# A hybrid decoder layer on one core: first token tiles on ScalarE's queue, one gate half moved forward, token loads four ahead, MLP operand copies pinned in program order

## The chip, the cores and the metric

The kernel runs on one core of a Trainium2 chip. The metric is the device time of one execution in microseconds, lower being better; the times shown are medians of several runs. The core has TensorE (matmuls; weight loads are listed apart as PEld), VectorE (DVE), ScalarE (ACT), GpSimd (POOL) and SyncE (SP). SP, ScalarE and GpSimd each have a queue on which they issue DMAs.

## The reference, cut to what matters

One layer of a decoder, batch 1, 512 tokens, model width 1024, f32:

```python
h = rms_norm(x, norm_mix)
rq, rk, rv, rg, cq, ckv, krope, gr, gm = split(h @ w_in)
a_ret = (rms_norm(retention(rope(rq), rope(rk) / 16, rv)) * silu(rg)) @ w_br   # 4 heads
q  = rms_norm(cq) @ w_uq;  k, v = split(rms_norm(ckv) @ w_ukv)                 # 8 heads
a_mla = causal_attention(rope(rms_norm(q)), rope(rms_norm([k, krope])), v) @ w_bm
x = x + (sigmoid(gr) * a_ret + sigmoid(gm) * a_mla) @ w_o
x = x + square(relu(rms_norm(x) @ w_up)) @ w_down                              # 4096 wide
x = x + sigmoid(rms_norm(x) @ w_ple_gate) * (p @ w_ple)
```

## The kernel before, in words

**Number format.** Every f32 operand is split into a high part (ScalarE rounds it, `ACT(hi, ..., AF.Copy)`) and a low part (VectorE subtracts: `lo = raw - hi`). A product is three matmuls: low weights by high tokens, high by low and high by high (`mm3`, line 292; all matmuls are issued through line 169). So each weight chunk costs a DMA (`prepare`, 218), a ScalarE copy (`wh`, line 262) and a VectorE subtraction (`wl`, 266), and each activation the same pair in `split` (302 to 314).

**Order of the work.** `step(key, fn, ...)` calls at the end of the kernel write the program's order; `run_steps` (271) walks them, and at each step that needs a weight chunk it converts chunks up to one ahead (AHEAD = 1) and starts DMAs up to three ahead (PREP = 3). Converted chunks share NW = 3 buffers, raw ones NRAW = 6. A planner then orders each engine's instructions: by program order among those that it takes to be ready by its own costs. `MM` pins all matmuls in program order. `tc.keep_in_program_order(i)` pins an instruction behind the one written just before it for the same engine; before the change it holds on ScalarE for the first chunks (`a1`), the first tokens, sines and sigmoids.

**Stages that the change touches.**
- The head (361 to 392): nine matmuls on a zero tile (364), then for k = 0 to 7 a weight chunk `a1 k` and a token tile `xs[k]`, both loaded on SP's queue in turn, the gains `gn` on ScalarE's queue, then constants and positions on SP's. `first_products` (385) multiplies them into three PSUM banks `pA`.
- The attention (1193 to 1271). Between its short dependent parts lie 26 fillers, halves of the gate products `gm` and `gr` (`gate_m` 679, `gate_r` 889); `fill(n)` places the next n of them, and the last call places what is left. The first half of a gate opens a PSUM bank, the second half scales it and sends it to DRAM on GpSimd's queue. Around the change the order is `query_rotary` (pqa, pqb), `mask_parts`, `rotary_out` (VectorE work on pqa and pqb), two fillers, `rotary_key` (it begins with the transposes `prho`), one filler, and so on.
- The bm stage (1272 to 1280): `norm_x` (708) loads token tile k once more on SP's queue, scales and splits it; it is called once ahead of every `branch_m` step.
- The MLP (1349 to 1395): group 0 of `up` in plain form, then groups in a seven-product form. `down` of group g and `up_seven` of group g+1 alternate in the order "1 v3 7 u1 2 6 u7 5 4 u6 3 u2 u5 u4": a bare number p is a down product (`dn`, two chunks of 24 matmuls in all), `up` a product of the next group (`us`, 48 matmuls, two chunks). `up_operand(p)` (996) makes the tokens of product p (`xu p`) and is called after "2", "5", "4", "3" and "u2" for p = 6, 2, 5, 4 and 3. `down_out` (1095) copies p = 1, 7, 6, 3 of group 0 out of PSUM on ScalarE (`d`, 1103). `up_seven` copies p = 1, 7, 6 out on ScalarE (`f`, 1042).

Of the kernel before, what the change touches and what calls it, by code (L numbers as in the profile page):

```python
# [33 lines left out]
AF = mybir.ActivationFunctionType  # L34
# [3 lines left out]
P = 128  # L38
# [110 lines left out]
def trunk_layer(ctx: ExitStack, tc: tile.TileContext, xT, pT, pos, gains, const, decay, wstream, outT):  # L149
    nc = tc.nc  # L150
# [15 lines left out]
    ACT = nc.scalar.activation  # L166

    def MM(*a, **k):
        return tc.keep_in_program_order(nc.tensor.matmul(*a, **k))  # L169

    def T(name, dtype=F32):
        return dyn.tile([P, S], dtype, tag="t", name=name)

    def K(name, dtype=F32):
        return keep.tile([P, S], dtype, tag="k", name=name)

    def B(name):
        return psum.tile([P, S], F32, tag="ps", name=name)
# [5 lines left out]
    gn = cpool.tile([P, G_N], F32, tag="gn", name="gn")  # L184
# [8 lines left out]
    def g(col):  # L193
        return gn[:, col:col + 1]
# [13 lines left out]
    def step(key, fn, *args):  # L208
        steps.append((key, fn, args))
# [8 lines left out]
    def prepare(key):  # L218

        if key[0] == "sw":  # L220
            _, blk, p, c = key

            def more(raw, kb, fb):
                nc.gpsimd.dma_start(raw, chunk(("w", blk, kb, fb, c)), accum_op=ALU.add)  # L224

            if p in (6, 4):
                return more(dw[blk, "t", c], *((0, 0) if p == 6 else (1, 0)))
            kb, fb = {1: (0, 0), 7: (0, 1), 2: (1, 0), 5: (0, 1), 3: (1, 1)}[p]
            nm = f"{blk[0]}{blk[1]}{p}{c}"
            if p == 7 and blk[0] in ("dn", "up"):  # L230
                raw = tail_pool["w"].tile([P, 1024], F32, tag="draw", name="dr_" + nm, bufs=NDRAW)
            else:
                raw = wpool.tile([P, 1024], F32, tag="wraw", name="wr_" + nm, bufs=NRAW)
            nc.sync.dma_start(raw, chunk(("w", blk, kb, fb, c)))
            dw[blk, "t" if p == 7 else p, c] = raw
            if p == 7:
                more(raw, 1, 1)
            elif p == 5:
                more(raw, 0, 0)
            return  # L240
        width = spec[key][0]
        nm = "_".join(str(x) for x in key)
        raw = wpool.tile([P, width], F32, tag="wraw", name="wr_" + nm, padded_shape=[P, 1024], bufs=NRAW)
        tc.keep_in_program_order(nc.sync.dma_start(raw, chunk(key))) if key[0] == "a1" else nc.sync.dma_start(raw, chunk(key))
        dw[key] = raw

    def load_chunk(key):

        sign = 1.0
        if key[0] == "sw":  # L250
            _, blk, p, c = key
            raw = dw[blk, "t" if p in (7, 6, 4) else p, c]
            nm = f"{blk[0]}{blk[1]}{p}{c}"
            if p in (1, 4) and blk[0] not in ("dn", "up"):
                sign = -1.0
        else:
            raw = dw[key]
            nm = "_".join(str(x) for x in key)
        width = raw.shape[-1]
        hi = wpool.tile([P, width], F32R, tag="whi", name="wh_" + nm, padded_shape=[P, 1024])  # L260
        lo = wpool.tile([P, width], F32R, tag="wlo", name="wl_" + nm, padded_shape=[P, 1024])
        i = ACT(hi, raw, AF.Copy, scale=sign)  # L262
        if key[0] == "a1":
            tc.keep_in_program_order(i)
        if sign > 0:
            TT(lo, raw, hi.bitcast(F32), op=ALU.subtract)  # L266
        else:
            STT(lo, raw, sign, hi.bitcast(F32), op0=ALU.mult, op1=ALU.subtract)
        wt[key] = (hi, lo)
# [22 lines left out]
    def mm3(ps, stat, mov, first, last, **k):  # L292

        (sh, sl), (mh, ml) = stat, mov
        MM(ps, sl, mh, start=first, stop=False, **k)
        MM(ps, sh, ml, start=False, stop=False, **k)
        MM(ps, sh, mh, start=False, stop=last, **k)

    def cut(pair, a, n=P):
        return pair[0][:, a:a + n], pair[1][:, a:a + n]  # L300

    def split(src, name, scale=None, hi=None, lo=None, pin=False):

        hi = T(name + "h", F32R) if hi is None else hi
        lo = T(name + "l", F32R) if lo is None else lo
        if scale is None:
            ACT(hi, src, AF.Copy)
            TT(lo, src, hi.bitcast(F32), op=ALU.subtract)  # L308
        else:
            i = ACT(hi, src, AF.Copy, scale=scale)  # L310
            if pin:
                tc.keep_in_program_order(i)
            STT(lo, src, scale, hi.bitcast(F32), op0=ALU.mult, op1=ALU.subtract)  # L313
        return hi, lo
# [35 lines left out]
    V = {}  # L350
# [10 lines left out]
    zero = K("zero", F32R)  # L361
    nc.vector.memset(zero.bitcast(F32), 0.0)
    ps = B("zero")
    for i in range(9):
        MM(ps, zero[:, 0:P], zero, start=i == 0, stop=i == 8)
    xs, xg = [], []
    for k in range(8):
        xs.append(T(f"x{k}"))
        if k < 6:
            prepare(("a1", k))  # L370
        tc.keep_in_program_order(nc.sync.dma_start(xs[k], xT[:, k]))
    nc.scalar.dma_start(gn, gains)
    tc.keep_in_program_order(nc.sync.dma_start(cst, const))
    tc.keep_in_program_order(nc.sync.dma_start(posi, pos.partition_broadcast(P)))
    for k in range(8):
        if k >= 6:
            prepare(("a1", k))
        load_chunk(("a1", k))
        xg.append(split(xs[k], f"xg{k}", g(G_MIX + k), pin=True))
# [5 lines left out]
    def first_products(w, k):  # L385
        if k == 0:
            V["pA"] = [B(f"pA{n}") for n in range(3)]
        for n in range(3):
            mm3(V["pA"][n], cut(w, n * P), xg[k], k == 0, k == 7)
        ACT(xs[k], xs[k], AF.Square)  # L390
        if k:
            TT(xs[0], xs[0], xs[k], op=ALU.add)
# [312 lines left out]

    xr, xn, XS = [], [], {}

    def norm_x(k):

        t = T(f"xr{k}")  # L710
        nc.sync.dma_start(t, xT[:, k])
        STT(t, t, g(G_MIX + k), V["rbc"], op0=ALU.mult, op1=ALU.mult)
        xr.append(t)
        xn.append(split(t, f"xn{k}"))

    def x_operand(p):
# [239 lines left out]
    def A(name, shape, tag, bufs, dtype=F32):  # L956
        return tail_pool["a"].tile([P, *shape], dtype, tag=tag, name=name, bufs=bufs)
# [38 lines left out]
    def up_operand(p):  # L996

        f1, f2 = F["x", 0], F["x", 1]
        a11, a21, a12, a22 = f1[:, :, 0:256], f1[:, :, 256:512], f2[:, :, 0:256], f2[:, :, 256:512]
        if p == 7:  # L1000
            TT(a11, a21, a11, op=ALU.subtract)
        elif p == 6:
            TT(a11, a22, a11, op=ALU.subtract)
            TT(a21, a21, a22, op=ALU.subtract)
        elif p == 3:
            TT(a11, a12, a11, op=ALU.subtract)
        src = {1: a11, 7: a11, 6: a11, 3: a11, 2: a12, 5: a21, 4: a22}[p]
        scale = -1.0 if p in (1, 4) else None
        XU[p], pairs = [], ([], [])
        for i, tiles in enumerate(pairs):  # L1010
            nm = f"xu{p}{'hl'[i]}"
            if p in (1, 7) or (p, i) == (6, 0):
                t = A(nm, (4, 256), "xs", 5, F32R)
                tiles.extend((t[:, 0:2], t[:, 2:4]))
                continue
            for c in range(2):

                t = K(f"{nm}{c}", F32R) if p != 6 else keep.tile([P, S], F32R, tag=("sum", "bc")[c], name=f"{nm}{c}", bufs=1)
                tiles.append(t.rearrange("p (k c) -> p k c", k=2))
        for c, (hi, lo) in enumerate(zip(*pairs)):  # L1020
            split(src[:, 2 * c:2 * c + 2], None, scale, hi=hi, lo=lo)
            XU[p].extend((hi[:, k], lo[:, k]) for k in range(2))

    def up_seven(w, gg, p, c):
# [159 lines left out]
    def fill(n=1):  # L1184
        for _ in range(n):
            if fillers and fillers[0][0] is None:
                step(*fillers.pop(0))
            if fillers:
                step(*fillers.pop(0))

    for k in range(8):
        step(("a1", k), first_products, k)
# [13 lines left out]
    step(None, gate_out, 0)  # L1206
    step(("qr", 0), query_rotary, 0)
    step(None, mask_parts)
    step(None, rotary_out, 0)
    fill(2)  # L1210
    step(None, rotary_key)
# [10 lines left out]
    for h in range(MH):  # L1222
        p, more = h // 2, h + 2 < MH
# [45 lines left out]
    step(None, attend, MH - 1)  # L1269
    step(None, mo_split, MH - 2)  # L1270
    fill(len(fillers))
    step(None, norm_x, 0)
    step(None, norm_x, 1)
    step(None, mo_split, MH - 1)
    for n in range(8):
        step(("bm", n), branch_m, n)
        if n < 6:
            step(None, norm_x, 2 + n)
        if n == 3:
            step(None, x_operand, 7)  # L1280
# [87 lines left out]
    for gg in range(GROUPS):  # L1368
        last, quarter = gg + 1 == GROUPS, 0
        for s_ in "1 v3 7 2 e 6 e 5 4 3".split() if last else seq:  # L1370
# [5 lines left out]
            elif s_[0] in "uv":  # L1376
                g_, p = gg + (s_[0] == "u"), int(s_[1])
# [4 lines left out]
            else:  # L1382
                p = int(s_)
# [74 lines left out]
```

## Time and profile before

| | |
|---|---|
| median of 3 runs | 1102.07 us (1100.86 to 1102.21) |
| profiled execution | 1101.0 us |
| its span, first to last instruction | 1099.2 us |
| granted TensorE clock, mean | 0.999 |
| ScalarE busy in the span | 51% |
| HBM traffic over the span | 175 GB/s |

The profile page gives each engine's busy time as a share of the span. A row of the timeline has the start in us from the span's start, the duration in us, the engine (a q behind it: its queue), the line of the kernel, the operation, the output and its inputs by their names in the program, the shapes, the count of instructions merged, and in brackets how long the engine was idle just before and what ended that. The table of waits has: the waiting engine, its tile and line, what released it, then total us, times, and the longest.

### The profile page before, as it was taken

How to read it: one execution, taken by the hardware profiler on the slowest of the kernel's cores; microseconds unless marked ns; L12 is line 12 of the kernel's file. 1: busy time of each engine (PE TensorE's matmuls, PEld its weight loads, DVE VectorE, ACT ScalarE, POOL GpSimd, SP SyncE). 2: the span in 40 equal slices, each digit the busy share in tenths (PEclk: the TensorE clock that was granted, in tenths of full speed). 3: DMA queues.
4: the chain of work that ended last, by engine and by line, in shares of the span. 5: the costliest groups of instructions: out<-in, count | busy, mean ns of one | idle time of the engine just before them, and what ended most of it. 6: DMA issues, size and time to landing. Idle time of an engine off the chain costs nothing. (4 is left out here: it accounts for less than half of the span.)

```text
span 1099.2 us, 14887 instructions
## 1 busy us (share of the span) xinstructions
PE 1085.2 (99%) x5569; PEld 923.3 (84%) x5569; DVE 757.9 (69%) x1176; ACT 565.8 (51%) x817; POOL 111.1 (10%) x145
## 2 busy tenths in 40 slices
PE   9999999999999999999999999999999999999998
PEld 7778888888888888888888888887899899898887
DVE  7697677566774655655465467649869769769784
ACT  7647656444466545344554644426645545546541
POOL 0000000000112001122100100011111111201000
PEclk9999999999999999999999999999999999999999
DMA  7232231356778744498864934694998999979511
GB/s 261 71 120 87 72 107 50 133 199 212 206 190 241 193 157 159 121 196 213 204 205 118 286 126 148 199 305 117 229 267 222 229 272 220 238 217 279 154 47 58
DMA packets 64616, 195.91 MB, mean 178 GB/s; under 512 B 7904, under 2 KB 9312, under 8 KB 64160
## 3 DMA queue, kind: packets, MB, share of 16 engines
q1 hardware_dynamic: 46464, 134.90, 35.7%
q0 software_dynamic: 17936, 60.04, 27.3%
q8 instruction: 44, 0.72, 0.3%
q14 instruction: 28, 0.23, 0.1%
q10 hardware_dynamic: 144, 0.03, 0.0%
HBM read 175.80 MB, written 17.04 MB: 175 GB/s over the span
## 5 line engine op out<-in xcount | busy, mean ns | idle before, releaser
L169 PE MATMUL dn<-wl_dn,ch 128*128 128x512 f32 x224 | 87.7, 391 | 1.5 <-DVE wl_dn L266 1.5
L169 PE MATMUL dn<-wh_dn,cl 128*128 128x512 f32 x224 | 87.7, 391 | 1.4 <-DVE cl L308 0.9
L169 PE MATMUL dn<-wh_dn,ch 128*128 128x512 f32 x224 | 87.2, 389 | 0.0
L262 ACT ACTIVATE wh_up<-wr_up 128x1024 fp32r<-128x1024 f32 x32 | 33.9, 1058 | 44.1 <-PE us L169 13.4
L266 DVE TENSOR_TENSOR wl_up<-wr_up,wh_up 128x1024 fp32r<-128x1024 f32 x32 | 39.1, 1221 | 24.4 <-ACT wh_up L262 24.0
L262 ACT ACTIVATE wh_dn<-wr_dn 128x1024 fp32r<-128x1024 f32 x32 | 33.9, 1059 | 34.1 <-PE us L169 16.5
L169 PEld LDWEIGHTS dn<-wh_dn,cl 128*128 128x128 f32 x224 | 42.1, 188 | 10.5 <-DVE cl L308 1.3
L169 PEld LDWEIGHTS dn<-wl_dn,ch 128*128 128x128 f32 x224 | 42.1, 188 | 10.3 <-DVE wl_dn L266 2.3
L169 PEld LDWEIGHTS dn<-wh_dn,ch 128*128 128x128 f32 x224 | 42.1, 188 | 8.8
L266 DVE TENSOR_TENSOR wl_dn<-wr_dn,wh_dn 128x1024 fp32r<-128x1024 f32 x32 | 39.0, 1220 | 10.7 <-ACT wh_dn L262 10.6
L262 ACT ACTIVATE wh_rv<-wr_rv 128x1024 fp32r<-128x1024 f32 x28 | 29.7, 1059 | 30.6 <-issue 9.9
L262 ACT ACTIVATE wh_rg<-wr_rg 128x1024 fp32r<-128x1024 f32 x28 | 29.6, 1059 | 30.4 <-PE rg L169 12.1
L266 DVE TENSOR_TENSOR wl_rg<-wr_rg,wh_rg 128x1024 fp32r<-128x1024 f32 x20 | 24.5, 1226 | 23.5 <-ACT wh_rg L262 23.4
L224 POOL DMA_DIRECT2D dr_dn<-wstream x24 | 21.9, 957 | 173.2 <-DVE rx L331 95.9
L266 DVE TENSOR_TENSOR wl_dn<-dr_dn,wh_dn 128x1024 fp32r<-128x1024 f32 x24 | 29.3, 1220 | 13.9 <-ACT wh_dn L262 13.9
L266 DVE TENSOR_TENSOR wl_rv<-wr_rv,wh_rv 128x1024 fp32r<-128x1024 f32 x20 | 24.4, 1223 | 16.2 <-ACT wh_rv L262 16.2
L266 DVE TENSOR_TENSOR wl_br<-wr_br,wh_br 128x1024 fp32r<-128x1024 f32 x16 | 19.5, 1221 | 19.7 <-ACT wh_br L262 19.7
L1105 DVE TENSOR_TENSOR d<-d,dn 128x1024 f32<-128x1024 f32 x24 | 29.2, 1217 | 5.4 <-PE dn L169 5.4
L262 ACT ACTIVATE wh_up<-dr_up 128x1024 fp32r<-128x1024 f32 x18 | 19.1, 1062 | 25.9 <-PE dn L169 14.1
L262 ACT ACTIVATE wh_dn<-dr_dn 128x1024 fp32r<-128x1024 f32 x24 | 25.3, 1053 | 13.1 <-PE dn L169 6.5
L262 ACT ACTIVATE wh_br<-wr_br 128x1024 fp32r<-128x1024 f32 x16 | 16.9, 1058 | 21.0 <-issue 12.8
L873 ACT ACTIVATE rt<-br 128x512 f32<-128x512 f32 x24 | 13.9, 594 | 25.8 <-PE br L169 25.8
(1889 smaller groups left out, 3690.2 us busy)
## 6 DMA issues: line engine op xcount, KB each, us to landing
wr_up<-wstream SPq DMA_DIRECT2D x32, 512.0 KB, 5.6
wr_dn<-wstream SPq DMA_DIRECT2D x32, 512.0 KB, 6.9
dr_dn<-wstream POOLq DMA_DIRECT2D x24, 512.0 KB, 9.5
wr_rv<-wstream SPq DMA_DIRECT2D x20, 512.0 KB, 4.1
wr_rg<-wstream SPq DMA_DIRECT2D x20, 512.0 KB, 5.0
dr_up<-wstream POOLq DMA_DIRECT2D x18, 512.0 KB, 9.0
wr_rv<-wstream POOLq DMA_DIRECT2D x16, 512.0 KB, 6.5
wr_rg<-wstream POOLq DMA_DIRECT2D x16, 512.0 KB, 6.9
```

What stands on the lines that cost most here:

```text
L169: return tc.keep_in_program_order(nc.tensor.matmul(*a, **k))
L224: nc.gpsimd.dma_start(raw, chunk(("w", blk, kb, fb, c)), accum_op=ALU.add)
L262: i = ACT(hi, raw, AF.Copy, scale=sign)
L266: TT(lo, raw, hi.bitcast(F32), op=ALU.subtract)
L873: ACT(t, ps, AF.Copy)
L1105: TT(to, to, dps[p], op=ALU.add if sign > 0 else ALU.subtract)
```

## The change

Five edits. (1) Token tiles 0 and 1 are loaded on ScalarE's queue instead of SP's, the gains on SP's behind the first chunk, and eight instead of nine zero matmuls run. (2) The first chunk's nine products run by kind (three of low weights, three of high by high, three of high by low) instead of by PSUM bank. (3) One filler moves to the place between `mask_parts` and `rotary_out`, so every later `fill` takes the following half. (4) The token loads of `norm_x` become a step of their own, four issued ahead of the first `norm_x` and one ahead of each of the first four `branch_m`. (5) In the MLP the ScalarE copies of all chunks of group 0 of `down` and group 1 of `up`, and the high parts of `up_operand` for p = 6, 2, 5, 4 and 3, are kept in program order.

```diff
@@ load_chunk
         i = ACT(hi, raw, AF.Copy, scale=sign)
-        if key[0] == "a1":
+        if key[0] == "a1" or key[0] == "sw" and key[1] in (("dn", 0), ("up", 1)):
             tc.keep_in_program_order(i)
@@ split
         if scale is None:
-            ACT(hi, src, AF.Copy)
+            i = ACT(hi, src, AF.Copy)
+            if pin:
+                tc.keep_in_program_order(i)
@@ head
-    for i in range(9):
-        MM(ps, zero[:, 0:P], zero, start=i == 0, stop=i == 8)
+    for i in range(8):
+        MM(ps, zero[:, 0:P], zero, start=i == 0, stop=i == 7)
...
-        tc.keep_in_program_order(nc.sync.dma_start(xs[k], xT[:, k]))
-    nc.scalar.dma_start(gn, gains)
+        tc.keep_in_program_order((nc.sync if k > 1 else nc.scalar).dma_start(xs[k], xT[:, k]))
+        if k == 0:
+            tc.keep_in_program_order(nc.sync.dma_start(gn, gains))
@@ first_products
-        for n in range(3):
-            mm3(V["pA"][n], cut(w, n * P), xg[k], k == 0, k == 7)
+        if k == 0:
+
+            (wh, wl), (xh, xl) = w, xg[k]
+            for i, (stat, mov) in enumerate(((wl, xh), (wh, xh), (wh, xl))):
+                for n in range(3):
+                    MM(V["pA"][n], stat[:, n * P:n * P + P], mov, start=i == 0, stop=False)
+        else:
+            for n in range(3):
+                mm3(V["pA"][n], cut(w, n * P), xg[k], False, k == 7)
@@ norm_x
+    def load_x(k):
+        xr.append(T(f"xr{k}"))
+        nc.sync.dma_start(xr[k], xT[:, k])
+
     def norm_x(k):
 
-        t = T(f"xr{k}")
-        nc.sync.dma_start(t, xT[:, k])
+        t = xr[k]
         STT(t, t, g(G_MIX + k), V["rbc"], op0=ALU.mult, op1=ALU.mult)
-        xr.append(t)
@@ up_operand
-            split(src[:, 2 * c:2 * c + 2], None, scale, hi=hi, lo=lo)
+            split(src[:, 2 * c:2 * c + 2], None, scale, hi=hi, lo=lo, pin=p not in (1, 7))
@@ steps
     step(None, mask_parts)
+    fill(1)
     step(None, rotary_out, 0)
...
     fill(len(fillers))
+    for k in range(4):
+        step(None, load_x, k)
     step(None, norm_x, 0)
...
     for n in range(8):
+        if n < 4:
+            step(None, load_x, 4 + n)
         step(("bm", n), branch_m, n)
```

## The prediction, made before the changed kernel ran

> **What bounds the kernel now.** I read the page first, then TensorE's waits, then the timeline around each wait, engine by engine, and last the table by stretches of time.
>
> ```profile
> PE 1085.2 (99%) x5569; PEld 923.3 (84%) x5569; DVE 757.9 (69%) x1176; ACT 565.8 (51%) x817; POOL 111.1 (10%) x145
> ```
>
> TensorE is busy in 99% of the span; the matmuls are issued in the written order and none is taken out (but for one warm-up matmul). So the change can win only where TensorE waits, and those places are few:
>
> ```profile
> PE gm L169 <- DVE wl_gm L266: 1.6, 1, 1.6
> PE dn L169 <- DVE wl_dn L266: 1.5, 1, 1.5
> PE zero L169 <- DVE zero L362: 1.5, 1, 1.5
> PE dn L169 <- DVE cl L308: 0.9, 1, 0.9
> PE sc L169 <- ACT sqk L527: 0.8, 1, 0.8
> PE pt0a L169 <- DVE p L653: 0.6, 1, 0.6
> PE gm L169 <- DVE mx L644: 0.6, 1, 0.6
> PE us L169 <- DVE wl_up L266: 0.6, 1, 0.6
> PE dn L169 <- ACT wh_dn L262: 0.5, 1, 0.5
> PE pA L169 <- DVE xg1l L313: 0.3, 1, 0.3
> PE pA L169 <- ACT xg1h L310: 0.2, 1, 0.2
> ```
>
> Columns: us in total, times, longest. Without the one at the very start these are 7.6 us in ten waits. Each also empties the pipe: a matmul lasts 0.39 us but the next starts 0.23 us after it (rows at 66.59 and 66.82 below), so a wait costs 0.16 us more than its idle time. Ceiling for any reordering: 7.6 + 10 x 0.16 = 9.2 us, plus the warm-up matmul. The sum below is made against the profiled execution, 1101.0 us (span 1099.2 and 1.8 around it); the median of the runs, 1102.07, lies 1.07 higher, and I add that at the end. A difference of 0.2% (2.2 us) is about the least that a measurement of this kernel can tell from none.
>
> **Part one: the head.**
>
> ```profile
> 1.46 4.21 PE L169 MATMUL zero<-zero 128*128 128x512 f32 x9 [1.46 <-DVE zero L362]
> 5.46 0.47 PE L169 MATMUL pA<-xg0h,wl_a 128*128 128x512 f32 x1
> ```
> ```profile
> 0.73 0.41 ACTq L372 DMA_DIRECT2D gn<-gains  x1
> 1.17 1.28 ACT L262 ACT_TABLE_LOAD   x1 [1.17 <-PEq L1451]
> 3.23 0.52 ACT L262 ACTIVATE wh_a<-wr_a 128x384 fp32r<-128x384 f32 x1 [0.78 <-DMA wr_a<-wstream]
> 4.12 0.72 ACT L310 ACTIVATE xg0h<-x,gn 128x512 fp32r<-128x512 f32 x1 [0.36 <-DMA x<-xT]
> 6.24 0.53 ACT L262 ACTIVATE wh_a<-wr_a 128x384 fp32r<-128x384 f32 x1 [1.40 <-DMA wr_a<-wstream]
> 7.14 0.72 ACT L310 ACTIVATE xg1h<-x,gn 128x512 fp32r<-128x512 f32 x1 [0.38 <-DMA x<-xT]
> ```
> ```profile
> 2.12 0.43 SPq L371 DMA_DIRECT2D x<-xT  x1
> ```
> ```profile
> 3.50:6.50 3.00, 3.00 (x11) 2.21 (x10) 1.31 (x2) 1.24 (x3) 0.00 (x0) 1.00 0.75 186
> 6.50:9.50 3.00, 2.56 (x10) 1.58 (x9) 1.91 (x4) 2.31 (x5) 0.00 (x0) 1.00 1.01 351
> ```
>
> Nine warm-up matmuls take 4.0 us from 1.46 to 5.46, 0.44 each. xg0h ends at 4.12 + 0.72 = 4.84, so with eight of them the first product can start near 5.03: 0.43 sooner at most. ScalarE's two token issues (0.41 each, where gn's one stood) push the table load from 1.17 to about 1.6, done at 2.9; it is covered by the wait of 0.78 before 3.23. The gains go to SP behind the first chunk; xg0h needs them, and they have until 4.12. The new order in the first chunk (all wl products, then wh, then the low tokens) needs xg0l only at the seventh matmul.
>
> But the second chunk decides. TensorE waits 0.2 and 0.3 there (with refill 0.8 in all), because wr_a is waited for 1.40 us and then the token tile 0.38. Tile 1 is issued at about 1.15 instead of 2.12, yet it takes its bytes from the same transfers: between 3.5 and 6.5 they move 186 GB/s at a share of 0.75. Best end: two streams fill that share and the pair is a microsecond earlier, gain 0.43 + 0.8 = 1.2. Worst end: tile 1 lands first, the weight chunk last, and its copy of 0.53 then stands in front of xg1h's 0.72: 0.5 lost. I take -0.2, near the row with the idle share, since the bytes that the pair needs are the same. The Trainium skill, in "DMA: Bandwidth & Descriptors", section "Issuing engines are not separate DMA queues", says that transfers from several engines run on the same 16 DMA engines and that only the time to issue is saved; by that rule this part is 0 and the sum below 0.2 smaller.
>
> **Part two: the gate half.**
>
> ```profile
> 66.59 0.39 PE L169 MATMUL gm<-xg7h,wh_gm 128*128 128x512 f32 x1
> 66.82 0.60 PE L169 MATMUL prho<-cst,rho 128*128 128x128 f32 x4
> 68.98 0.47 PE L169 MATMUL gm<-xg0h,wl_gm 128*128 128x512 f32 x1 [1.56 <-DVE wl_gm L266]
> ```
> ```profile
> 68.15 0.68 DVE L266 TENSOR_TENSOR wl_gm<-wr_gm,wh_gm 128x512 fp32r<-128x512 f32 x1
> ```
>
> The moved fill puts one more gate half (12 matmuls x 0.23 = 2.7 us) ahead of everything from rotary_key on, and the last fill has one less. Its weight chunk, its copies and, every second half, its product with rbc and its store on POOL's queue come earlier too; those are off the path. TensorE's order is now gm1 both halves, gm2 first half, then prho. VectorE still makes wl_gm of gm2 behind rotary_out's work, at 68.15, so the wait at 68.98 stays, and prho's 0.60 us, which lay inside it, comes behind: with 0.16 overlapped, +0.44. What wins is the shift itself: prho, the sums, the head factors and the scores come 2.7 us later for TensorE, while the softmax of head 0 keeps its time. The wait of pt0a (0.6) and the bank wait of sc (0.8) fall inside that: -(0.76 + 0.96) = -1.7. The gm wait on mx (0.6) is for a PSUM bank where a first half opens; after the shift a second half stands there and needs none, but another place then opens one: half of 0.76, -0.4. At the end head 7's attend loses half its cover; in my reading the copies there finish just in time, so 0, at worst +0.4. Sum -1.7; ends -2.1 to +0.8.
>
> **Part three: token loads.**
>
> ```profile
> 231.00:275.00 44.00, 44.00 (x197) 36.47 (x196) 28.16 (x42) 19.13 (x27) 3.72 (x7) 1.00 0.68 223
> 755.00:786.00 31.00, 28.34 (x144) 23.23 (x143) 31.00 (x34) 24.02 (x29) 6.08 (x7) 1.00 0.78 192
> ```
>
> Columns: length, then busy PE, PEld, DVE, ACT, POOL, clock, DMA share, GB/s. In the bm stage (first row) TensorE is busy 44.00 of 44.00, so what norm_x gains has nothing to shorten. The cover is the stage's own matmuls. Eight issues on SP pass up to four bm or rq chunks and zm reloads; with a DMA share of 0.68 they fit. 0; ends -0.1 to +0.4 (a tile slot late, weight chunks queued behind it).
>
> **Part four: the pins.** The second row above: in the MLP's first stage VectorE is busy 31.00 of 31.00 us and TensorE loses 2.7. Among VectorE's work there:
>
> ```profile
> 758.40 1.28 DVE L308 TENSOR_TENSOR xu2l<-x2n,xu2h 128x512 fp32r<-128x512 f32 x2
> 759.61 1.28 DVE L308 TENSOR_TENSOR xu5l<-x2n,xu5h 128x512 fp32r<-128x512 f32 x2
> 760.81 0.68 DVE L313 SCALAR_TENSOR_TENSOR xu4l<-x2n,xu4h 128x512 fp32r<-128x512 f32 x1
> 761.42 1.28 DVE L984 SCALAR_TENSOR_TENSOR f<-up,bcx 128x512 f32<-128x512 f32 x2
> 762.62 1.21 DVE L266 TENSOR_TENSOR wl_dn<-dr_dn,wh_dn 128x1024 fp32r<-128x1024 f32 x1
> ```
>
> The first three are operands for products 40 us later. Pinning their high parts behind the weight copies sends them back, and wl_dn comes 3.0 us (758.40 to 761.42) sooner; it then ends at 760.8, when TensorE asks for it. The three waits go: 0.5 + 1.5 + 0.6 + 3 x 0.16 = -3.1; next late is nothing until the pins themselves.
>
> For a pin puts a copy behind whatever ScalarE instruction was written before it, and four times that one waits for TensorE:
>
> ```profile
> 815.00 1.03 ACT L1103 ACTIVATE d<-dn 128x1024 f32<-128x1024 f32 x1 [1.66 <-PE dn L169]
> 815.92 1.05 ACT L262 ACTIVATE wh_up<-wr_up 128x1024 fp32r<-128x1024 f32 x1
> ```
> ```profile
> 759.74 1.14 ACT L310 ACTIVATE xu4h<-x2n 128x512 fp32r<-128x512 f32 x2
> ```
> ```profile
> 803.74 5.75 PE us L169 x48
> 809.49 5.47 PE dn L169 x24
> 814.96 17.27 PE us L169 x144
> ```
>
> The second chunk of u1 is copied behind d of dn7, that of u7 behind d of dn6: from the end of dn, d takes 0.92 (815.00 to 815.92), the copy 1.05, wl 1.21, together 3.2, while TensorE fills 5.75 / 2 = 2.88 less the 0.16 of overlap: 0.5 each. The second chunk of dn3 stands behind f of u6 (of d's size): 3.2 against 2.73, 0.45. The second chunk of u2 stands behind d of dn3 and both halves of xu4h (1.04 without overlap): 0.92 + 1.04 + 1.05 + 1.21 = 4.2 against 2.72: 1.5. Behind each waiting copy are queued the wl on VectorE and TensorE itself, so all of it counts: +3.0. Net -0.1; ends -3.1 to +3.0.
>
> **Sum.** -0.2 - 1.7 + 0 - 0.1 = -2.0: 1099.0 by the profiled execution, 1100.1 as a median.
>
> **Rivals.** (a) *The pins cost nothing*: the instruction ahead of each of the four copies is done before TensorE's last matmul of the chunk. Then part four gives -3.1: 1097.1. For it: these are four places out of some thirty pinned copies, and I read their neighbours from the written order alone. Against it: d at 815.00 ends a wait of 1.66 us for just that matmul. Chance 0.26. (b) *Slower: the pins cost 3.0 and remove nothing*, because VectorE's backlog comes from x2n and the f and s work, which are not pinned, so wl_dn stays as late as now. Place: 755 to 820. 1100.1 + 3.1 = 1103.2; with the gate half's lower end (+0.8 for -1.7) 1105.7. It decides as soon as the relief at wl_dn is under 1 us. For it: 31.00 of 31.00. Against it: the five rows above. Chance 0.20, a little over half of it beyond 0.2%. (c) *The gate half does not do what it says*: PSUM banks bind one place later and the two waits are met again. 1100.1 + 1.7 = 1101.8. Chance 0.09. (d) *The warm-up is one matmul short*: if the first token tile or the gains are late, TensorE stands idle after the eighth and the slow rate of 0.44 lasts for another 4.0 us, nine matmuls x 0.21 = 1.9: 1102.0. The Trainium skill, in "TensorE: Matmul & The Clock Gate", section "Part 1: The HAM clock gate", states that the rate follows a window of recent activity and no count of matmuls; by that rule the eighth suffices if no gap opens. Chance 0.05.
>
> **How the numbers follow.** The forecast, 1100.1 (1098.6 to 1101.6 alone), has 0.40; half of it is faster by over 0.2%, under 1099.9. Faster 0.20 + 0.26 = 0.46. Slower, over 1104.3: 0.12 of (b) and 0.02 of (d), 0.14. The rest, 0.40, is within 0.2%. The range from 1096.3 ((a) with the head's best end nearly whole) to 1104.5 leaves out 2 in 10.
>
> **What would show it.** Right: eight zero matmuls, pA from about 5.05, TensorE still held at the second chunk; wl_gm still ends its wait near 68.7 and prho follows the gate half; no wait at pt0a; in 755 to 770 xu2l, xu5l, xu4l gone from VectorE and no wait on wl_dn; new waits of us on wl_up near 769, 786 and, at 1.5, near 815. Wrong: those new waits absent, or wl_dn waits as long as now, or any wait over 0.5 us between 181 and 716.

## The result, and the profile after

The changed kernel takes 1105.61 us (median of 22 runs, 1102.28 to 1107.98), the kernel before beside it 1102.05 (22 runs, 1100.86 to 1103.90): a ratio of 1.0032, 95% interval 1.0025 to 1.0039. It is slower by 3.6 us. The forecast was 1100.1, the range ended at 1104.5.

The profiled execution of the changed kernel took 1103.96 us with a span of 1102.2, so between the two profiles the loss is 3.0 of those 3.6 us. The first line of the page shows where it is not:

```profile
PE 1086.2 (99%) x5568; PEld 924.2 (84%) x5568; DVE 756.1 (69%) x1176; ACT 566.0 (51%) x817; POOL 111.4 (10%) x145
```

No engine has more instructions than before, and there is one matmul less. What changed is where TensorE waits. Its waits (us in total, times, longest):

```profile
PE us L169 <- DVE wl_up L266: 2.6, 3, 1.5
PE mo L169 <- DVE mx L654: 2.3, 1, 2.3
PE gm L169 <- DVE wl_gm L266: 1.9, 1, 1.9
PE zero L169 <- DVE zero L364: 1.5, 1, 1.5
PE dn L169 <- DVE cl L310: 0.9, 1, 0.9
PE sc L169 <- ACT sqk L537: 0.7, 1, 0.7
PE pA L169 <- ACT xg0h L312: 0.6, 1, 0.6
PE dn L169 <- DVE wl_dn L266: 0.4, 1, 0.4
PE pbk L169 <- DVE hr L614: 0.2, 1, 0.2
```

Against the list of before: the waits for p (pt0a), for wh_dn and for mx at a gate product are gone, and that for wl_dn is down from 1.5 to 0.4. In their place stand 2.3 at mo, 2.6 in three waits for wl_up where one of 0.6 was, and 1.9 for wl_gm where 1.6 was. Without the one at the very start, before had 7.6 us of waits and after has 9.6.

How far TensorE is behind the kernel before at the first matmul of each stage, by the start times of the profiles, is worked out below (us; the runs named e... are the experiments of the next section; us0 and us1 are the first matmuls of u1 and u7, dn4 is the first of the next group of down). In pt0a and pt3a of after, e2 and, for pt0a only, e7, the number holds 2.7 us of the moved gate half itself, which the stage bm has back.

```
first matmul of   before   after   e2     e7     e12    e6     e10    e13
pA (tokens)         5.46   +0.36  +0.00  +0.00  +0.09  -0.50  +0.06  +0.09
pqa (rotary)       57.16   +0.36  -0.39  -0.11  -0.92  -0.16  -1.34  -0.95
pt0a (head 0)      97.39   +3.13  +3.96  +2.59  -0.91  -0.20  -0.42  -0.98
pt3a (head 3)     154.96   +4.71  +5.53  -0.03  -0.93  -0.24  -0.43  -1.03
bm                231.12   +2.16  +3.01  -0.03  -0.92  -0.25  -0.42  -1.03
dn0 (MLP)         755.63   +2.40  +3.12  +6.93  -0.52  +0.32  -0.42  -0.81
us0               770.16   -0.93  +4.29  +5.76  -3.87  -3.03  -3.90  -4.15
us1               786.92   +0.46  +4.19  +5.75  -1.70  -0.40  -3.68  -0.10
dn4               832.07   +2.94  +4.19  +5.75  +0.82  -0.33  -3.62  -0.02
end              1099.23   +2.96  +4.24  +5.81  +0.87  +1.21  -3.59  +1.79
```

So in the profile the head costs 0.36, the stretch with the gate half 1.80 (from +0.36 to +2.16), the stages of the early token loads nothing (+2.16 from bm to up), and the MLP 0.80.

**The head.** ScalarE's timeline and then TensorE's, of the changed kernel:

```profile
4.28 0.52 ACT L262 ACTIVATE wh_a<-wr_a 128x384 fp32r<-128x384 f32 x1 [1.34 <-DMA wr_a<-wstream]
5.05 0.72 ACT L312 ACTIVATE xg0h<-x,gn 128x512 fp32r<-128x512 f32 x1 [0.24 <-DMA gn<-gains]
```
```profile
4.18 1.06 PE L169 MATMUL zero<-zero 128*128 128x512 f32 x2
5.82 0.79 PE L169 MATMUL pA<-xg0h,wl_a 128*128 128x512 f32 x1 [0.58 <-ACT xg0h L312]
```

The first weight chunk is copied at 4.28 instead of 3.23 and xg0h at 5.05 instead of 4.12; the wait named at the end of the second line is for the gains, which now come behind the first chunk. TensorE stands still for 0.58 us after the eighth warm-up matmul, and the full granted clock begins at 9.52 us where it began at 5.62 before; until then the products start 0.43 us apart.

**The gate half.** TensorE's timeline where it waits for wl_gm, and where mo begins:

```profile
66.95 0.39 PE L169 MATMUL gm<-xg7h,wh_gm 128*128 128x512 f32 x1
69.26 0.50 PE L169 MATMUL gm<-xg0h,wl_gm 128*128 128x512 f32 x1 [1.92 <-DVE wl_gm L266]
...
148.25 0.28 PE L169 MATMUL pv<-wh_v,ckv1h 128*128 128x256 f32 x1
150.87 0.47 PE L169 MATMUL mo<-ath,v10l 128*128 128x512 f32 x1 [2.35 <-DVE mx L654]
```

The kernel before, at the same work:

```profile
145.36 0.40 PE L169 MATMUL mo<-ath,v10l 128*128 128x512 f32 x1
...
147.17 0.28 PE L169 MATMUL mo<-ath,v11h 128*128 128x256 f32 x1
148.09 0.47 PE L169 MATMUL gm<-xg0h,wl_gm 128*128 128x512 f32 x1 [0.65 <-DVE mx L644]
```

In both kernels TensorE waits for the same thing, the first maximum of head 3's scores, which frees a PSUM bank. Before, the twelve mo matmuls (1.8 us, 145.36 to 147.17) run ahead of the matmul that needs the bank; after, mo itself needs it. VectorE's first maximum in the two kernels, before and after:

```profile
147.66 0.28 DVE L644 CUSTOM_DVE_ANT_0 p<-sc,kf 128x128 f32<-128x128 f32 x1
```
```profile
150.43 0.28 DVE L654 CUSTOM_DVE_ANT_0 p<-sc,kf 128x128 f32<-128x128 f32 x1
```

The matmuls that follow the scores start at 141.39 and 144.40 in these profiles, so the maximum comes 6.3 and 6.0 us behind the scores: VectorE is not slower, TensorE asks one place earlier.

**The MLP.** VectorE's timeline of the changed kernel, for the five rows of before that the prediction showed, and the row of the stage from 755 to 786:

```profile
757.22 1.22 DVE L1015 TENSOR_TENSOR x2n<-x2n,x2n 128x1024 f32<-128x1024 f32 x1
758.35 1.22 DVE L1016 TENSOR_TENSOR x2n<-x2n,x2n 128x1024 f32<-128x1024 f32 x1
759.49 1.22 DVE L266 TENSOR_TENSOR wl_dn<-wr_dn,wh_dn 128x1024 fp32r<-128x1024 f32 x1
760.62 1.28 DVE L996 SCALAR_TENSOR_TENSOR f<-up,bcx 128x512 f32<-128x512 f32 x2
761.82 1.22 DVE L266 TENSOR_TENSOR wl_dn<-dr_dn,wh_dn 128x1024 fp32r<-128x1024 f32 x1
```
```profile
755.00:786.00 31.00, 30.55 (x157) 25.74 (x156) 26.62 (x26) 19.85 (x21) 5.24 (x6) 1.00 0.77 188
```

xu2l, xu5l and xu4l are gone from here, VectorE has 26.62 us of work instead of 31.00, and TensorE loses 0.45 instead of 2.66. That is the gain of the pins. What they cost shows in four waits between 772 and 821 us; for the longest, ScalarE first and then TensorE:

```profile
816.20 1.03 ACT L1115 ACTIVATE d<-dn 128x1024 f32<-128x1024 f32 x1 [3.22 <-PE dn L169]
817.12 1.14 ACT L312 ACTIVATE xu4h<-x2n 128x512 fp32r<-128x512 f32 x2
818.16 1.99 ACT L262 ACTIVATE wh_up<-wr_up 128x1024 fp32r<-128x1024 f32 x2
```
```profile
820.52 0.39 PE L169 MATMUL us<-xu2h,wl_up 128*128 128x256 f32 x1 [1.49 <-DVE wl_up L266]
```

The copy of the weight chunk stands behind d, which waits for TensorE, and behind xu4h: the chain the prediction wrote down, with its 1.5.

### The profile page after: what moved, and what is told of

Its sections match the earlier page's. It is cut to its first block, busy times and chain, and to the rows that moved or that the text cites. A ratio compares the mean times of both kernels' runs of the same rounds, so it can differ in the third digit from the quotient of the medians.

```text
span 1102.2 us, 14868 instructions
## 1 busy us (share of the span) xinstructions
PE 1086.2 (99%) x5568; PEld 924.2 (84%) x5568; DVE 756.1 (69%) x1176; ACT 566.0 (51%) x817; POOL 111.4 (10%) x145
## 4 chain that ended last, share of the span: by engine, by line
PE 87%; DVE 5%; DMA 4%; ACT 2%; issue 1%; SPq 0%; POOL 0%; ACTq 0%; POOLq 0%; DVEq 0%
PE dn L169 11%; PE us L169 10%; PE br L169 8%; PE rv L169 7%; PE rg L169 7%; PE pg L169 4%; PE gr L169 4%; PE rk L169 4%; PE bm L169 4%; PE rq L169 4%; PE wo L169 4%; PE gm L169 3%; PE ro L169 2%; PE sc L169 2%; DMA x2n<-x2d 2%; PE pA L169 2%
```

## The experiments

Each kernel was compared with the kernel before on the same chip; times are medians of 6 to 12 runs, and each kernel has one profile.

**Theory**: the gate half and the pins of the weight chunks cost more than they give. **Rivals**: the head costs it (idle TensorE, late warm-up); or the four parts harm one another and none does alone. Four kernels with one part each.

**e1, the head alone**: the two edits of setup and of first_products as in the diff, with eight zero matmuls.

> Only the head's edits: two token tiles on ScalarE's queue, gains on SP's, eight zero matmuls, the first chunk's products by kind. Theory A (the traces' account adds up part by part): first product at 5.8 instead of 5.46, nine slow matmuls behind it, the second chunk unhindered, all in all +0.4 us (1102.4 to 1102.5) in every run, as tight as the kernel before. Theory B (the head also upsets the clock, differently from run to run): runs spread over several us, 1102 to 1107, median +2, with mean clocks under 0.999, and this part carries most of the 1.6 us by which the changed kernel's median lies above its own profiled execution.

Measured 1100.82 (before 1101.56), ratio 0.9991 (0.9982 to 0.9999). The head by itself gains about a microsecond; it is not the loss. The stage pcq starts 1.3 us earlier than before in its profile.

**e2, the gate half alone**:

```
     step(None, mask_parts)
+    fill(1)
     step(None, rotary_out, 0)
```

> Only the gate half moved ahead of rotary_out. Theory A: prho falls out of the wait at 67 (+0.4), the wait of pt0a goes (-0.8), a wait of 2.3 us for a PSUM bank comes at head 1's attend near 148 and the gm wait of 0.6 there goes: +1.8 in all by the start of the bm stage, 1103.9, no spread. Theory B (the two long waits, 1.9 and 2.3 us, let the clock drop): spread over several us and a median of +3 or more. My forecast before the result was -1.7, 1100.3.

Measured 1105.73, ratio 1.0035 (1.0023 to 1.0048): this one line loses as much as the whole change. Its profile has the waits of the changed kernel (1.92 for wl_gm, 2.35 at mo) and one thing more. The table by stretches of 3.41 us around the first of them (length, busy PE, PEld, DVE, ACT, POOL, granted clock, DMA share, GB/s):

```profile
61.73:65.14 3.41, 3.41 (x17) 2.83 (x16) 3.41 (x7) 2.44 (x5) 0.71 (x1) 1.00 0.19 77
65.14:68.55 3.41, 1.49 (x8) 0.91 (x6) 3.41 (x7) 1.74 (x3) 0.00 (x0) 1.00 0.08 19
68.55:71.96 3.41, 3.41 (x8) 2.73 (x9) 3.35 (x6) 0.00 (x0) 0.56 (x1) 0.50 0.54 151
71.96:75.38 3.42, 3.42 (x18) 2.79 (x18) 2.48 (x5) 0.63 (x1) 0.00 (x0) 1.00 0.48 137
```

After the wait the granted clock is 0.50 for one stretch, and eight matmuls run in it where 15 would (3.41 / 0.227): about 1.6 us more. A second such stretch stands at 768. The wait thus costs its own length and, in some executions, the clock behind it.

**e3, the pins alone** (weight chunks and operands, as in the diff).

> Only the pins of the MLP's ScalarE copies. Theory A: the wait on VectorE's backlog goes (-3.3 from the first down product to the next), new waits of 0.6, 0.8, 0.5 and 1.6 us on the chunks behind d and f come, +0.5 to +0.8 in all: 1102.7, tight. Rival (the pins are a gain and the other parts spoil it): 1099 to 1100.

Measured 1103.23, ratio 1.0018 (1.0009 to 1.0027). The four waits of the prediction are all there (0.6, 0.9, 0.5 and 1.65 us of lost time), and with them waits for wl_dn at 782 (0.9) and 863 to 867 (1.0 and 0.9) that neither the prediction nor the changed kernel has.

**e4, the early token loads alone.**

> Only the token loads four ahead. Theory A: TensorE never waits in the bm stage, so 1102.1, no change, though norm_x is done earlier on VectorE. Rival (the loads displace chunk loads on SP's queue or tile slots): +0.5 or more, with a wait on wl_bm or wl_rq.

Measured 1102.08, ratio 1.0006 (0.9997 to 1.0015): no difference that can be told. The four ratios add up to +0.50%, while the whole change costs 0.32%: the parts do not simply add. The waits of e3 that the changed kernel's profile lacks come to 2.8 us.

The second round asks for the mechanism of each loss. **e5**: is the wait for wl_gm there because the chunk is written behind the rotary work? Both fills ahead, TensorE's order as before:

```
+    fill(2)
     step(None, rotary_out, 0)
-    fill(2)
```

> The kernel before with its fill(2) moved ahead of the rotary queries instead of behind them: TensorE's order is unchanged, only the load of the next gate half's weights is written ahead of the rotary work on VectorE and ScalarE. If TensorE waited 1.56 us for wl_gm near 69 us because that load stands behind the rotary work, the wait goes, no clock drop can follow it, and the median falls by 1.5 to 2 us (about 1100.0). If the time only moves on to what the rotary work holds up (transposes, pt0a), a new wait of 1 us or more shows between 69 and 105 us and the median stays within 0.5 us of before.

Measured 1109.22, ratio 1.0066 (1.0054 to 1.0078), the slowest of all. TensorE's waits in it:

```profile
PE sqr L169 <- DVE sa L562: 2.8, 1, 2.8
PE st L169 <- ACT sums L589: 1.9, 1, 1.9
```

The wait for wl_gm (1.6) is gone and two others of 4.7 have come: the rotary work, written behind two more loads that wait for their buffers, starts at 67.83 on VectorE instead of 63.11. The granted clock drops twice behind them.

**e9**: the same load in the middle of rotary_out, behind the sum sa and ahead of the splits, so that sa is not held up.

```
         TT(sa, sa, sb, op=ALU.add)
+        V["sa"], V["o"] = sa, (o1, o2)
+
+    def rotary_parts(gq):
+        o1, o2 = V["o"]
         h1, l1 = split(o1, f"qr1{gq}")
...
     step(None, rotary_out, 0)
     fill(2)
+    step(None, rotary_parts, 0)
```

> The kernel before with its fill(2) moved into the middle of the rotary queries: behind the sum of squares sa, ahead of the two splits and their DMAs. TensorE's order is unchanged. If the earlier run with both fills ahead lost its time because sa came late, and only that, sa is here in time (no wait at sqr over 0.3 us), the wait for wl_gm near 69 us falls from 1.56 to under 0.3 us, and the median is 1 to 1.8 us under before. If VectorE's or ScalarE's whole backlog is what TensorE waits for in the end, a wait of 1 us or more comes at st, pt0a or sc and the median is within 0.5 us of before.

Measured 1103.04, ratio 1.0012 (1.0004 to 1.0021). sqr no longer waits; the list has

```profile
PE st L169 <- ACT sums L592: 1.4, 1, 1.4
...
PE gm L169 <- DVE wl_gm L266: 0.9, 1, 0.9
```

0.7 saved at wl_gm, 1.4 paid at st. Between 62 and 80 us these loads can be moved, but each place found so far holds something else up.

**e7**: the PSUM bank theory of the wait at mo. With one gate half more ahead, the halves that open a bank and those that do not have changed places in everything that follows. Here the half is moved ahead as in e2, and one filler is dropped behind head 2's transposes, so that from there they fall as before:

```
-            if h:
+            if h > 2:
                 fill(1)
             if h == 2:
                 step(None, rotary_out, 1)
```

> The gate half alone ahead of the rotary queries, as in the earlier run of that part, but the filler half behind head 2's transposes is dropped, so that from there the halves fall at the same places as in the kernel before. PSUM bank theory: the 2.35 us wait of mo for VectorE's mx near 148 us comes from the halves having changed places from there on, so it goes, a wait of about 0.6 us at the gate matmuls near 147 comes back, and the median is 1.2 to 2.2 us under that run's 1105.7. Rival: VectorE is late there by itself because of the rotary work; the wait of 2 us or more stays at mo or its neighbour and the median stays within 0.8 us of 1105.7.

TensorE's timeline at mo:

```profile
145.55 0.40 PE L169 MATMUL mo<-ath,v10l 128*128 128x512 f32 x1
...
147.36 0.28 PE L169 MATMUL mo<-ath,v11h 128*128 128x256 f32 x1
148.06 0.47 PE L169 MATMUL gm<-xg0h,wl_gm 128*128 128x512 f32 x1 [0.42 <-DVE mx L644]
```

The 2.35 us at mo are gone and 0.42 at gm are back, as the theory has it; TensorE is level with before at pt3a and stays so to 708 us (-0.03 in the table). The time, 1104.44, ratio 1.0032 (1.0019 to 1.0044), is only 1.3 under e2's: in its profile TensorE waits 0.8 for xr at 710 and 4.0 for wl_up at 746, behind two loads of x2n that land some 5 us later than before. Why they do is open. **e11** makes the same edit in the whole changed kernel.

> The changed kernel with one filler half fewer behind head 2's transposes, so that from there the gate halves fall as in the kernel before. By the PSUM bank theory TensorE's wait of 2.35 us at mo near 148 us goes, 0.4 to 0.6 us at gm comes back, and the median is 1.5 to 2.2 us under the changed kernel's 1105.6: 1103.4 to 1104.1. Rival: the changed kernel's loss lies elsewhere and the median stays above 1105.

Measured 1103.46, ratio 1.0017 (1.0008 to 1.0026) where the changed kernel has 1.0032: 1.65 us back. From pqa to bm its profile loses 0.10 us where that of the changed kernel loses 1.80; these 1.7 are the bank's share. In the median they are mixed with two other things: the wait for xr at 710 that e7 has stands here too (0.8), and the mean granted clock of its runs is higher (0.9990, the changed kernel 0.9980).

**e12**, the changed kernel without the gate half:

> The changed kernel without the gate half ahead of the rotary queries. If the gate half is the main loss, the median falls by 3 to 4.5 us, to 1101.1 to 1102.6, and the waits at gm near 67 us (1.9) and mo near 148 us (2.35) are gone, 1.56 us at gm behind prho back. If the pins lose as much as the gate half, the median stays at 1103 or more.

Measured 1101.87, ratio 0.9999 (0.9990 to 1.0008). Without that one line the change costs nothing: the gate half is the loss, 0.33% or 3.6 us. Its profile keeps the pins' gain and their price (from -0.52 at dn0 to -3.87 at us0, then up to +0.82 at dn4).

**e6**: are the four waits due to the pinned chunks alone? On the kernel before, the operands are pinned and the condition on the chunks stays as it was:

```
-            split(src[:, 2 * c:2 * c + 2], None, scale, hi=hi, lo=lo)
+            split(src[:, 2 * c:2 * c + 2], None, scale, hi=hi, lo=lo, pin=p not in (1, 7))
```

> The kernel before with only the MLP operands' engines and places pinned; the up chunks stay where the planner has them. Theory: the pins of the operands remove the VectorE backlog at 755 to 770 us (3.6 us of TensorE excess there), and the four waits of the full pins (u1c1 0.6, u7c1 0.8, dn3c1 0.5, u2c1 1.6) come from the pinned chunks alone: then none of the four shows, and the median falls by 2.5 to 4 us (1097.5 to 1099). Rival: the pinned operands by themselves displace the chunks, two or more of the four waits show again, and the median is within 1 us of before.

Measured 1100.74, ratio 0.9988 (0.9979 to 0.9997). Three of the four waits are gone (u1c1, dn3c1, u2c1; c1 is a product's second chunk), TensorE is 3.0 ahead at us0, and by us1 it has lost 2.6 of it: waits for wl_dn at 778 and 782 (0.6 and 1.0) and for wl_up at 785 (0.9). Both theories were half right.

**e8, e10, e13, e14** put edits together. e8: the head with nine zero matmuls, both fills ahead as in e5, operand pins.

> Head edits with nine zero matmuls, the two gate halves both ahead of the rotary queries, and the pins of the operands without the chunks. If each of the three theories holds by itself, no TensorE wait over 1.2 us is left between 6 us and the tail, the granted clock shows no drop after its start, and the median is 1096 to 1097.5 with a spread under 2 us. If waits only change places, the median is 1099 or more and a wait of 1.5 us or more shows at another matmul.

Measured 1102.82, ratio 1.0022 (1.0010 to 1.0034): the waits at sqr and st (2.8 and 1.9) are e5's again, and the clock drops behind the first. e10: the head with eight, the load of e9, operand pins.

> The head edits (eight zero matmuls), the load in the middle of the rotary queries and the pins of the operands alone, on the kernel before. If the three gains stand apart from one another, the median is 1098 to 1099.5. If what is gained ahead of 760 us is lost again to the weight stream at 778 to 786 us, the waits for wl_dn and wl_up there add up to 3 us or more and the median is over 1100.

Measured 1099.32 (before 1101.89), ratio 0.9976 (0.9966 to 0.9986): faster than both kernels. e13 is e10 without the load of e9.

> The head edits (eight zero matmuls) and the pins of the operands alone on the kernel before, without the load in the middle of the rotary queries. If that load costs 0.8 us by itself and nothing else hangs on it, the median is 0.6 to 1.2 us under the 1099.3 of the run with it (1098.1 to 1098.7). If the microsecond that it adds ahead of 760 us only gives the weight stream at 778 to 786 us time to arrive, the two waits for wl_dn and the one for wl_up there come back (2 us and more) and the median is 1099.5 to 1101.

Measured 1100.56 (before 1101.53), ratio 0.9984 (0.9972 to 0.9995), with runs from 1096.07 to 1102.88. ScalarE's timeline in e13 and in e10, and the stretch from 766 to 790 of each:

```profile
777.15 1.06 ACT L262 ACTIVATE wh_dn<-dr_dn 128x1024 fp32r<-128x1024 f32 x1 [4.17 <-DMA dr_dn<-wstream]
...
780.96 1.06 ACT L262 ACTIVATE wh_dn<-dr_dn 128x1024 fp32r<-128x1024 f32 x1 [1.71 <-DMA dr_dn<-wstream]
```
```profile
773.49 1.06 ACT L262 ACTIVATE wh_dn<-dr_dn 128x1024 fp32r<-128x1024 f32 x1 [0.25 <-DMA dr_dn<-wstream]
...
777.37 1.06 ACT L262 ACTIVATE wh_dn<-dr_dn 128x1024 fp32r<-128x1024 f32 x1 [1.78 <-DMA dr_dn<-wstream]
```
```profile
766.00:790.00 24.00, 20.92 (x123) 17.63 (x122) 16.79 (x16) 13.91 (x16) 4.97 (x6) 1.00 0.93 205
```
```profile
766.00:790.00 24.00, 23.85 (x151) 21.39 (x150) 19.39 (x18) 15.81 (x17) 3.45 (x4) 1.00 1.01 228
```

In e13 the weights land 3.7 us later than in e10 and TensorE loses 3.1 us of these 24, in e10 0.15. The share of the DMA engines is 0.93 and 1.01 (it counts whole packets by their start, so it can pass 1): once VectorE's backlog is out of the way, the weight transfers are the next to be late, and whether they are in time differs between these two profiles. Late weights come a second time, at 860 to 867: 1.5 us in e13, 0.9 in e14, 0.8 in e6, none in e10. The intervals of e10 and e13 overlap, so that the load of e9 is what brings the weights in time is not shown. e14, the changed kernel without the gate half and without the pinned chunks, says the same.

> The changed kernel without the gate half and without the pins of the chunks: its head, its early loads and its operand pins are left. If the pinned chunks cost what the four waits show and nothing else is late there, the median is 2 to 3.5 us under the 1101.9 of the run without the gate half alone (1098.4 to 1099.9). If the stream of the MLP weights is the next to be late, waits for wl_dn and wl_up of 1.5 to 2.5 us in sum take their place at 775 to 790 us and the median is 1100 to 1101.5.

Measured 1100.62 (before 1101.53), ratio 0.9992 (0.9983 to 1.0000); its waits for the weights at 777 to 786 are 0.99, 0.76 and 0.17.

## Why the prediction was wrong

**The ceiling and the reading of the waits** held: the loss, like every gain, is time in which TensorE waits. What it left out is that a wait has a price beyond its length plus 0.16 (the clock, below). Most of its signs of being right came true, among them no wait at pt0a and the new waits on wl_up; but none of its signs looked between 105 and 181 us, where mo waits.

**The head** (-0.2, ends -1.2 to +0.5) stayed inside its ends: alone it gave -1.0 (-2.0 to -0.1) by the ratio, and +0.36 in the profile of the changed kernel. The expected start near 5.05 was not met: 5.82 there, 5.41 to 5.70 in the others with this head and eight zero matmuls. The gains did not have the time that the prediction gave them, until 4.12: behind the first chunk they landed at 4.53 to 5.01. By rival (d) a gap behind the eighth warm-up matmul would leave the slow rate for 4.0 us more. The gap came, 0.58 us, and the first nine products of the changed kernel do start 0.43 apart from the second on; but TensorE was at pqa only 0.36 behind, mostly because xg1h was begun at 6.17 instead of 7.14 and the two waits of the second chunk were gone. A gap alone does not decide it: e8 has one of 0.66 us, and there the full clock began at 4.55, before it. The second pair came sooner at the cost of the first: in the eight kernels with this head the first chunk landed at 4.12 to 4.27 and xg1h began at 6.10 to 6.18, in the other eight at 3.20 to 3.31 and 6.85 to 7.14. Tile 0 too is issued sooner, at 0.73 instead of 1.18; which of the two tiles delays the chunk is not shown. With that agrees the rule of the Trainium skill, "DMA: Bandwidth & Descriptors", section "Issuing engines are not separate DMA queues", that transfers issued from several engines run on the same 16 DMA engines. Tile 1 was issued at 1.17 instead of 2.12, and its pair came sooner by about as much.

**The gate half** (-1.7, ends -2.1 to +0.8) is the step that failed; measured +1.8 in the profile and +3.6 by taking it out (e12). By its own terms, in lost time of TensorE including the refill:

- prho falling out of the wait, +0.44: the wait went from 1.72 to 2.09, +0.37. Right.
- pt0a, -0.76: right, that wait is gone. But the reason given was not: the softmax of head 0 does not "keep its time". Its first exponential starts at 96.54 instead of 93.62, 2.9 later, since what feeds it comes from TensorE behind the moved half. TensorE came later still by the waits ahead of it (0.37 at wl_gm, 0.29 at a new wait of pq).
- the bank wait of sc, -0.96: wrong, 0.97 became 0.89. It waits for sqk, which starts on ScalarE at 103.26 instead of 100.28, 3.0 later, exactly as much as TensorE at this place. A shift of everything changes no wait between two things that are both shifted.
- the gm wait on mx, -0.4: it went whole, -0.80, and mo took it over with 2.51. This is the mechanism that the prediction had as rival (c), "PSUM banks bind one place later", with a chance of 0.09, and priced at the gain that it would undo (1.7). They bind one place earlier, ahead of 1.8 us of matmuls that used to cover the wait, so that it costs another 1.7. Shown by e7 and e11, where the wait of 2.35 at mo goes when the halves fall as before.

These terms make +0.37 - 0.76 - 0.08 - 0.80 + 2.51, with 0.29 at pq and 0.18 at pbk: +1.7. The rest of the 3.6 is not in this pair of profiles, for in this execution the clock held. Over all runs the mean granted clock is 0.9980 for the changed kernel, 0.9993 for e12 and 0.9965 for e2; a clock lower by 0.0013 over 1100 us is 1.4 us. With that agrees that the three runs of the changed kernel at a mean clock of 1.000 took 1102.28 to 1103.96 us and the four at 0.996 took 1106.48 to 1107.98. No run changes the clock alone, so this share is worked out and not shown, and it leaves some 0.4 us of the 3.6 open.

**The token loads** (0): right.

**The pins** (-0.1, ends -3.1 to +3.0). Both sums were right in size, each read from the rows: the backlog gave back 3.3 where 3.1 was said, and the four waits took 0.6, 0.8, 0.5 and 1.65 where 0.5, 0.5, 0.45 and 1.5 were said, each at its chunk. In the changed kernel that nets +0.8 from up to the end; alone the pins cost 2.0 (1.0 to 3.0). What failed is the clause "next late is nothing until the pins themselves". e6, e13 and e14 show that the weight transfers are: with the pinned chunks' waits taken away, TensorE loses 2.4 us in e6 and 3.8 in e13, refill included, to the weights at 777 to 786, and only in e10 nearly nothing. The pins also give something that the sum has no term for: the clock drops behind the wait for wl_dn near 765 in three of the seven profiles without pinned operands (e1, e2, e5) and in none of the nine with them (that of e14 follows other waits, at 780). The mean clock of e12, 0.9993 against 0.9983 for the kernel before beside it, is worth about 1.1 us by the same estimate as above. Rival (b) had named 1105.7 for its worst case, close to the 1105.61 measured, but that is luck: its reason, no relief at wl_dn, did not come about, and only 0.8 us of the loss in the profile lies in the MLP.

The sum of the profile, -2.0, came out as +3.0; 3.5 of those 5.0 us are the gate half, 0.9 the pins, 0.56 the head.

## What to carry to other kernels

Work that is moved ahead in an in-order stream shifts its followers and those that feed them alike; count it as a gain only where one side stays where it is, and look up which of the two the row names. A kernel whose PSUM banks go round in the order of the program has a phase: moving one piece that opens a bank every second time changes who waits for every bank after it, so follow the ring to its end, with the work that stands ahead of each waiting matmul as its cover. And where a stall goes, read the next resource's share in the stretch behind it (DMA at 0.95 from 766 to 790 in before): that is what can take the gain, as in e6 and e13.

## What the runs showed of the hardware that was not expected

The granted clock falls in steps of 3.41 us counted from the moment at which its full rate began, and in the 16 profiles eight of the nine drops ahead of the kernel's end fit one condition: a stretch in which TensorE stood idle for more than about six tenths is followed by one at 0.50. In e2 the stretch 65.14 to 68.55 (1.49 busy) is followed by 0.50; the changed kernel waits just as long, but its steps cut that wait in two, and 1.69 of 3.41 busy leaves the clock as it is:

```profile
64.13:67.54 3.41, 3.21 (x15) 2.31 (x13) 3.41 (x7) 1.50 (x4) 0.00 (x0) 1.00 0.19 77
67.54:70.95 3.41, 1.69 (x7) 1.41 (x8) 3.41 (x7) 1.03 (x2) 0.23 (x1) 1.00 0.30 76
70.95:74.37 3.42, 3.42 (x18) 2.81 (x18) 3.36 (x7) 0.64 (x1) 0.34 (x1) 1.00 0.56 174
```

Counted from matmul start to matmul start, the eight stretches were 0.61 to 0.84 idle, and all that brought no drop 0.61 or less. The ninth drop does not fit: it follows the stretch 71.47 to 74.89 of e5, in which TensorE is busy 2.48 us, though much of it with the small matmuls of sqr and sums. And the edge is not sharp: in e11 the same wait leaves 1.48 of 3.41 busy, as in e2, and no drop follows. So a wait of about 2.1 us cost 1.6 us more in one profile (e2) and nothing in three (the changed kernel, e7, e11); where it falls explains the changed kernel and e7, not e11. The Trainium skill, "TensorE: Matmul & The Clock Gate", section "Part 1: The HAM clock gate", states a free-running window of 3413 ns, and that the slow state follows an idle window; the length agrees with the records here (3.41), but a window need not be idle throughout: 0.61 sufficed.

That the runs of one kernel lie 1.6 (e1) to 7.1 us (e8) apart fits this and the transfers of the MLP; how such a spread divides between the two was not measured, and why two transfers that are issued about 0.5 us apart sometimes end 2 us apart and sometimes almost at once (the ones issued at 757 in e10 and e13) stays open.
